# Hybrid encoder trunk on one core: attention weights of the third token group turned by VectorE's 32 by 32 block transposes and SBUF transfers instead of TensorE products

## The chip, the cores and the metric

The kernel runs on one core of a Trainium2 chip. The metric is the device time of one execution in microseconds (us). The engines are named as in the profile: PE is TensorE (PEld its weight loads), DVE is VectorE, ACT is ScalarE, POOL is GpSimd, SP is SyncE, which here only issues transfers; "SPq" is the issuing of one.

## What is computed

One layer of an encoder over 2048 prompt tokens and 8 x 16 sample tokens, width 1024, all in float32. One input projection feeds three branches (a short convolution, a gated linear recurrence, attention) and the merge gates; each branch is projected back, gated and added, and an output projection closes the layer. The part that the change touches is the attention of the prompt. It is "stick-breaking": no softmax, but for query q and key k (k before q) the weight is sigmoid(z) times the product of sigmoid(-z) over all keys between k and q.

```python
def sb_attend(q, k, v, q_pos, k_pos):
    z = jnp.einsum('bqhd,bkhd->bhqk', qf, kf) * (1.0 / math.sqrt(SB_DH))
    causal = (k_pos[None, :] < q_pos[:, None])[None, None]
    log_1mb = jnp.where(causal, jax.nn.log_sigmoid(-z), 0.0)
    rest = lax.cumsum(log_1mb, axis=3, reverse=True) - log_1mb
    A = jnp.where(causal, jnp.exp(jax.nn.log_sigmoid(z) + rest), 0.0)
    return jnp.einsum('bhqk,bkhd->bqhd', A, vf)
```

## The kernel before

Tokens come in 17 tiles of 128 (one of samples, 16 of the prompt), and the tiles in three groups (`GROUPS`, line 39). For each group, `run_jobs` (line 1319) goes through the columns of the input projection in jobs of 128 or 256 columns; each job is a chain of products into a PSUM buffer `acc` (lines 710 and 721), emptied by ScalarE or VectorE. After the third group comes the merge (`merge_jobs`, line 1398), whose products are at lines 1440 and 1471.

Other work is laid between these products by hand. Every generator that yields a cost is drained by a `Background` (line 58): after a few products of the main job the caller grants a budget, and the background runs until its yields have used it up. `hbg` runs the recurrence beside every group (`recurrence`, line 983): per pair of tiles and head seven levels, and in each VectorE makes two operands (`WR`, `WL`, lines 1028 and 1034) and updates `X` and `hgf` (1035, 1036), TensorE multiplies the operands into a PSUM buffer `z` (1039), and VectorE copies a masked part of that into the scores `sc` (1040). Before the first level VectorE multiplies `qk` (999), TensorE sums it into a `z`, and VectorE starts `sc` from it (1004). `bg` runs the attention of the prompt, beside the third group at rate 0.65 (0.3 of that in jobs of 256 columns) and beside the merge at rate 1.

The attention (`attn_pair`, line 297) takes 512 queries (four blocks of 128) and two heads at a time, from the latest keys back, in segments of up to 512 keys. For one segment and one head it makes a step, for each of the four query blocks a turn:

- TensorE: z = Q Kt in two products (lines 329, 330), into one of two `z` buffers, which the recurrence uses as well;
- ScalarE: sigmoid(-z) into one of three buffers `snb` (333), sigmoid(z) into one of four `sp` (335); on the diagonal GpSimd masks both (338);
- VectorE: the running product along the keys by a scan into one of two buffers `pr` (342), continued over segments through `carry` (346, GpSimd), then `sp` = `sp` x `pr` (347), the weights, with queries on partitions;
- three turns later (`queue`, `shorten`, `DEPTH`): TensorE turns the weights so that keys are on partitions, by one product with an identity per 128 x 128 block (line 310) into PSUM `tp`, and ScalarE copies them into `aT` (311).

When both heads of a segment are turned, `accumulate` (line 352) multiplies `aT` by the values `Vt` into the PSUM buffer `pv` (359). At the end of a pair of heads `store` (364) multiplies `pv` by a gate `ot` that was loaded from DRAM (320, 366), splits the result into two parts (`oth` and `ot`, in `store_parts`, line 178) and stores both to `OX` by SyncE.

All transfers but the indirect ones are issued from SyncE's queue. A tile framework places the waits and the order of each engine's instructions; eight semaphores, DMAHW0 to DMAHW7, are given to the transfers in turn.

Of the kernel before, what the change touches and what calls it, by code (L numbers as in the profile page):

```python
# [8 lines left out]
F32 = mybir.dt.float32  # L9
# [7 lines left out]
P = 128  # L17
# [81 lines left out]
def trunk(ctx: ExitStack, tc: tile.TileContext, x_prompt, x_sample, cache_conv, state_hgrn, cache_k, cache_v,  # L99
# [140 lines left out]
    at = None  # L240
    snb = []
    turn = [0]

    def open_attention():

        nonlocal at
        at = ctx.enter_context(tc.tile_pool(name="at", bufs=2, side="right"))

        for i in range(3):
            s = at.tile([P, 513], F32, name=f"snb{i}", bufs=1)  # L250
            nc.vector.memset(s[:, 512:513], 1.0)
            snb.append(s)


# [13 lines left out]
    def load_step(m):  # L268
# [20 lines left out]
        if e == 0:  # L289
            Vt = at.tile([P, 4, 2, 64], F32, tag="Vt", name="Vt")  # L290
            nc.sync.dma_start(Vt[:, :nb], VV[(1 + b0) * P:(1 + b1) * P, h:h + 2].rearrange(
                "(b p) e c -> p b e c", p=P))
        else:
            Vt = held[m - 1][3]
        held[m] = (Q1, Q2, Kt, Vt)

    def attn_pair(m0, m1):
# [8 lines left out]
        def transposed(i, e, w, sp, aT):  # L306
            nb = w // P
            tp = ps_tp()
            for j in range(nb):
                nc.tensor.transpose(tp[:, j * P:(j + 1) * P], sp[:, j * P:(j + 1) * P], idf)  # L310
            nc.scalar.copy(aT[:, e, 0:nb, i * P:(i + 1) * P], tp[:, :w].rearrange("p (b q) -> p b q", q=P))  # L311

        gate = []
        for m in range(m0, m1):
            _, _, si, last, b0, b1, e = steps[m]
            load_step(m)
            load_step(m + 1)
            if m == m1 - 1:
                gate.append(at.tile([P, 512], F32, tag="ot", name="ot", bufs=1))
                nc.sync.dma_start(gate[0][:, :n], SZ[pair][:, q0:q0 + n])  # L320
            Q1, Q2, Kt, Vt = held[m]
            nb = b1 - b0
            diag = si == 0
            if e == 0:
                aT = at.tile([P, 2, 4, 512], F32, tag="aT", name="aT", bufs=1)
            for i in range(nq):
# [25 lines left out]
            def accumulate(nb=nb, diag=diag, first=si == 0, last=last, Vt=Vt, aT=aT):  # L352
                if first:
                    box.append(ps_pv())
                pv = box[0]
                for j in range(nb):
                    c0 = j * P if diag else 0
                    for e in range(2):
                        nc.tensor.matmul(pv[64 * e:64 * e + 64, c0:n], Vt[:, j, e], aT[:, e, j, c0:n],  # L359
                                         start=first and j == 0, stop=last and j == nb - 1, skip_group_check=True)  # L360
# [1171 lines left out]
```

## Time and profile before

| what | us |
|---|---|
| time, median of 3 runs (2873.08 to 2874.37) | 2874.01 |
| the profiled execution: its own time | 2876.11 |
| its span, first to last instruction | 2873.2 |
| TensorE busy | 2853.0 |
| VectorE busy | 1546.5 |
| ScalarE busy | 1018.7 |
| GpSimd busy | 331.8 |

A row of a group reads: line, engine, operation, output <- input, shapes, count | busy us in all, mean ns of one | idle time of the engine just ahead of it, and what ended most of that. A matmul's busy time overlaps with its neighbours', so a group's busy time isn't what TensorE would save without it. A row by stretch gives its start and end, its length, each engine's busy us with the number of instructions, the clock granted to TensorE (1.00 is full), the mean busy share of the 16 DMA engines, and what they moved in GB/s. In the chain of waits a piece is work that the end of the run hung on. A row of transfers gives the issuing queue, the count, the size and the median time from issue to landing.

### The profile page before, as it was taken

Reading aid. Unit: us, or ns where it says so; the run is one execution under the profiler, and the core shown is the slowest. Engines: PE = TensorE matmul, PEld = TensorE weight load, DVE = VectorE, ACT = ScalarE, POOL = GpSimd, SP = SyncE. Lnnn points to the kernel's source line nnn. Section 1 sums busy time; section 2 is a strip of 40 time slices with the busy share of each in tenths; the row PEclk is TensorE's granted clock in tenths of the full one; section 3 lists DMA queues with packets and bytes.
Section 4 is the critical chain, followed back from the end, with each engine's and each line's share of the span. In section 5 each row is a group of like instructions: output and inputs, shape, how many; then the busy total and the mean of one; then the engine's idle time right before and its main releaser. Section 6 shows DMA issues by size and latency. Waiting matters only on the chain.

```text
span 2873.2 us, 51723 instructions
## 1 busy us (share of the span) xinstructions
PE 2853.0 (99%) x19479; PEld 2662.3 (93%) x19479; DVE 1546.5 (54%) x3304; ACT 1018.7 (35%) x2375; POOL 331.8 (12%) x802
## 2 busy tenths in 40 slices
PE   9999999999999999999999999999999999999999
PEld 9999999999999999999999999999998888787888
DVE  5454635641344442545434747557485876867743
ACT  4333222242233332213334444434444444544420
POOL 3110000111200000001323111111010011010100
PEclk9999999999999999999999999999999999999999
DMA  8887777777678887746766454544447877878876
GB/s 306 305 276 247 231 241 244 231 243 243 212 249 266 276 265 243 243 167 192 237 215 202 146 173 136 173 139 151 144 145 238 286 234 239 266 250 266 271 250 210
DMA packets 370475, 649.76 MB, mean 226 GB/s; under 512 B 33481, under 2 KB 246306, under 8 KB 339506
## 3 DMA queue, kind: packets, MB, share of 16 engines
q1 hardware_dynamic: 369458, 644.36, 68.2%
q8 instruction: 154, 2.52, 0.4%
q0 software_dynamic: 768, 2.10, 0.2%
q14 instruction: 95, 0.78, 0.1%
HBM read 447.06 MB, written 199.27 MB: 225 GB/s over the span
## 4 chain that ended last, share of the span: by engine, by line
PE 76%; DVE 2%; DMA 2%; issue 1%; ACT 0%; POOL 0%; SPq 0%; DVEq 0%; POOLq 0%; ACTq 0%
PE acc L710 33%; PE acc L721 10%; PE acc L1440 9%; PE acc L1471 6%; PE pv L359 4%; PE tp L310 4%; PE z L330 2%; PE z L329 2%; PE z L1039 1%; PE tp L458 1%; DMA gate<-GM 1%; PE pv L522 1%; PE z L476 0%; PE hg L1086 0%; PE hg L826 0%
## 5 line engine op out<-in xcount | busy, mean ns | idle before, releaser
L710 PE MATMUL acc<-hx,w 128*128 128x384 f32 (+1 forms) x6816 | 1251.8, 333 | 0.1
L710 PEld LDWEIGHTS acc<-hx,w 128*128 128x128 f32 x6816 | 1106.5, 188 | 21.9 <-issue 15.2
L721 PE MATMUL acc<-w,hx 128*128 128x256 f32 x2544 | 328.6, 284 | 1.8 <-DVE hx L176 0.9
L342 DVE TENSOR_TENSOR_SCAN pr<-snb,carry 128x513 f32<-128x513 f32 x192 | 246.5, 1284 | 153.3 <-ACT snb L333 151.7
L721 PEld LDWEIGHTS acc<-w,hx 128*128 128x128 f32 x2544 | 310.9, 188 | 5.0 <-DVE hx L176 1.7
L311 ACT COPY aT<-tp 128x512 f32<-128x512 f32 (+2 forms) x320 | 167.6, 524 | 375.2 <-PE tp L310 361.3
L710 PE MATMUL acc<-hx,wst 128*128 128x384 f32 x1248 | 247.2, 344 | 0.0
L1440 PE MATMUL acc<-o,w 128*128 128x512 f32 (+2 forms) x1080 | 234.7, 363 | 1.8 <-DMA o<-OX 1.8
L333 ACT ACTIVATE snb<-z 128x512 f32<-128x512 f32 (+2 forms) x320 | 172.4, 539 | 144.5 <-PE z L330 140.4
L710 PEld LDWEIGHTS acc<-hx,wst 128*128 128x128 f32 x1248 | 215.4, 188 | 6.4 <-issue 3.7
L1440 PEld LDWEIGHTS acc<-o,w 128*128 128x128 f32 x1080 | 185.1, 188 | 33.8 <-issue 5.3
L347 DVE TENSOR_TENSOR sp<-sp,pr 128x512 f32<-128x512 f32 (+2 forms) x320 | 195.3, 611 | 29.2 <-POOL sp L338 3.7
L342 DVE TENSOR_TENSOR_SCAN pr<-snb,one 128x129 f32<-128x129 f32 (+3 forms) x128 | 114.4, 894 | 123.9 <-POOL snb L338 123.6
L310 PE MATMUL tp<-idf,sp 128*128 128x128 f32 x1088 | 171.3, 273 | 2.5 <-ACT aT L311 1.5
L335 ACT ACTIVATE sp<-z 128x512 f32<-128x512 f32 (+2 forms) x320 | 171.5, 536 | 0.0
L1471 PE MATMUL acc<-w,mh 128*128 128x256 f32 x816 | 161.2, 285 | 1.0 <-DVE yt L1479 0.8
L1176 ACT ACTIVATE gm<-acc 128x384 f32<-128x384 f32 (+1 forms) x144 | 68.2, 474 | 230.4 <-PE acc L710 197.5
L310 PEld LDWEIGHTS tp<-idf,sp 128*128 128x128 f32 x1088 | 131.8, 141 | 19.3 <-issue 4.4
L176 DVE TENSOR_TENSOR w<-wst,w 128x1024 fp32r<-128x1024 f32 x72 | 88.1, 1223 | 110.7 <-ACT w L175 107.9
L1471 PEld LDWEIGHTS acc<-w,mh 128*128 128x128 f32 x816 | 131.0, 188 | 7.2 <-issue 4.2
L329 PE MATMUL z<-Kt,Q 128*128 128x512 f32 (+2 forms) x320 | 128.8, 403 | 0.3 <-ACT sp L335 0.2
L359 PE MATMUL pv<-aT,Vt 128*64 128x512 f32 (+3 forms) x640 | 128.1, 535 | 0.0
(299 smaller groups left out, 3570.1 us busy)
## 6 DMA issues: line engine op xcount, KB each, us to landing
w<-W SPq DMA_DIRECT2D x168, 1024.0 KB, 6.0
W<-w SPq DMA_DIRECT2D x72, 1024.0 KB, 5.0
wst<-W SPq DMA_DIRECT2D x112, 512.0 KB, 5.1
wst<-in_w_in_dram SPq DMA_DIRECT2D x72, 512.0 KB, 5.1
GM<-gm SPq DMA_DIRECT2D x120, 192.0 KB, 3.7
W<-mwp SPq DMA_DIRECT2D x40, 512.0 KB, 4.2
Kt<-KT SPq DMA_DIRECT2D x160, 128.0 KB, 3.1
o<-OX SPq DMA_DIRECT2D x72, 256.0 KB, 4.7
```

The costliest lines, as they stand in the source:

```text
L310: nc.tensor.transpose(tp[:, j * P:(j + 1) * P], sp[:, j * P:(j + 1) * P], idf)
L311: nc.scalar.copy(aT[:, e, 0:nb, i * P:(i + 1) * P], tp[:, :w].rearrange("p (b q) -> p b q", q=P))
L329: nc.tensor.matmul(z[:, :w], Q1[:, i * P:(i + 1) * P], Kt[:, :w], start=True, stop=False)
L333: nc.scalar.activation(sn[:, 512 - w:512], z[:, :w], AF.Sigmoid, scale=-0.125)
L335: nc.scalar.activation(sp[:, :w], z[:, :w], AF.Sigmoid, scale=0.125)
L342: nc.vector.tensor_tensor_scan(pr[:, 512 - w:513][:, ::-1], s_in, s_in, one if diag else carry[e][i], ALU.mult, ALU.bypass)
L347: nc.vector.tensor_tensor(sp[:, :w], sp[:, :w], pr[:, 513 - w:513], ALU.mult)
L359: nc.tensor.matmul(pv[64 * e:64 * e + 64, c0:n], Vt[:, j, e], aT[:, e, j, c0:n], start=first and j == 0, stop=last and j == nb - 1, skip_g ...
L710: nc.tensor.matmul(acc[:, :n], w[0][a][:, k], hT[b][:, k, :n], start=k == 0 and i == 0, stop=k == KB - 1 and i == 2)
L721: nc.tensor.matmul(acc[:, :256], hT[b][:, k, ti * P:(ti + 1) * P], w[k // 4][a][:, k % 4], start=k == 0 and i == 0, stop=k == KB - 1 and i ...
L1440: nc.tensor.matmul(acc[:, :n], w[0][a][:, k, dd * P:(dd + 1) * P], box[x][b][:, k, sl], start=k == 0 and i == 0, stop=k == 3 and i == 2)
L1471: nc.tensor.matmul(acc[:, :256], box["l" if b else "h"][:, k, ti * P:(ti + 1) * P], w[k // 4][a][:, k % 4], start=k == 0 and i == 0, stop= ...
```

## The change

In the third token group, not in the merge, the weights are turned in another way. VectorE transposes the 32 by 32 blocks of `sp` in place of TensorE, into a new buffer `T` (one, for the four turns of a step). That leaves each block turned, but not at the partitions where it belongs. So after the fourth turn 16 transfers, SBUF to SBUF, of 32 partitions each (64 KB) carry the blocks to their partitions in `aT`; eight are issued by ScalarE's queue, eight by SyncE's. `aT` has another layout for that, and in the merge ScalarE's copy writes this layout too.

Other things change with it. The accumulation of a segment waits in `pending` and joins the queue two turns into the next segment; the store as well; at the end of 512 queries a yield of 5.0 stands ahead of the rest. `Vt` has one buffer instead of two and is loaded in the third turn of the second head. The gate `ot` and the part `oth` no longer have buffers of their own but take those of `pr`, and the gate is loaded with the last accumulation. There are two buffers `snb` instead of three. Costs that the turns yield are the same as before.

```diff
-        for i in range(3):
+        for i in range(2):
             s = at.tile([P, 513], F32, name=f"snb{i}", bufs=1)
...
+        turned_.append(at.tile([P, 4, 4, 4, 32], F32, name="T", bufs=1))
+        nc.gpsimd.memset(turned_[0], 0.0)
...
-            nc.scalar.copy(aT[:, e, 0:nb, i * P:(i + 1) * P], tp[:, :w].rearrange("p (b q) -> p b q", q=P))
+            nc.scalar.copy(aT[:, e, i, :, 0:nb], tp[:, :w].rearrange("p (b a q) -> p a b q", a=4, q=32))
+
+        def turned_blocks(i, e, w, sp, aT):
+
+            T = turned_[0]
+            nc.vector.transpose(T[:, i, :, 0:w // P].rearrange("p c b q -> p b c q"),
+                                sp[:, :w].rearrange("p (b c q) -> p b c q", c=4, q=32))
+            if i == nq - 1:
+                for a in range(4):
+                    for c in range(4):
+                        queue_ = nc.scalar if (a + c) % 2 else nc.sync
+                        queue_.dma_start(aT[32 * c:32 * c + 32, e, :, a], T[32 * a:32 * a + 32, :, c])
...
-            if m == m1 - 1:
-                gate.append(at.tile([P, 512], F32, tag="ot", name="ot", bufs=1))
-                nc.sync.dma_start(gate[0][:, :n], SZ[pair][:, q0:q0 + n])
...
             if e == 0:
-                aT = at.tile([P, 2, 4, 512], F32, tag="aT", name="aT", bufs=1)
+                aT = at.tile([P, 2, 4, 4, 4, 32], F32, tag="aT", name="aT", bufs=1)
+                turn_ = turned_blocks if by_blocks[0] else transposed
+                if not by_blocks[0]:
+                    queue.extend(pending)
+                    pending.clear()
...
-                queue.append((True, lambda i=i, e=e, w=w, sp=sp, aT=aT: transposed(i, e, w, sp, aT)))
+                queue.append((True, lambda i=i, e=e, w=w, sp=sp, aT=aT, f=turn_: f(i, e, w, sp, aT)))
+                if e == 0 and i == 1:
+
+                    queue.extend(pending)
+                    pending.clear()
+                if e == 1 and i == 2:
+                    Vt = at.tile([P, 4, 2, 64], F32, tag="Vt", name="Vt", bufs=1)
...
+                if last:
+                    gate.append(at.tile([P, 513], F32, tag="pr", name="ot", bufs=2))
+                    nc.sync.dma_start(gate[0][:, :n], SZ[pair][:, q0:q0 + n])
...
-                        nc.tensor.matmul(pv[64 * e:64 * e + 64, c0:n], Vt[:, j, e], aT[:, e, j, c0:n],
+                        nc.tensor.matmul(pv[64 * e:64 * e + 64, c0:n], Vt[:, j, e],
+                                         aT[:, e, c0 // P:nq, :, j].rearrange("p i a q -> p (i a) q"),
                                          start=first and j == 0, stop=last and j == nb - 1, skip_group_check=True)
             if e:
-                queue.append((False, accumulate))
+                (pending if turn_ is turned_blocks else queue).append((False, accumulate))
...
-            th = at.tile([P, 512], F32, tag="oth", name="oth", bufs=1)
+            th = at.tile([P, 513], F32, tag="pr", name="oth", bufs=2)
             store_parts(OX[2, pair], slice(q0, q0 + n), t[:, :n], th[:, :n])
-        queue.append((False, store))
+        (pending if turn_ is turned_blocks else queue).append((False, store))
...
         yield from shorten(0)
+        if pending:
+            yield 5.0
+            queue.extend(pending)
+            pending.clear()
+            yield from shorten(0)
...
     tpools.close()
+    by_blocks[0] = False
```

In the changed kernel the lines above are numbered anew: 999, 1004, 1028, 1034, 1035, 1036, 1039 and 1040 of the recurrence become 1028, 1033, 1057, 1063, 1064, 1065, 1068 and 1069, the scan 354, the multiply 359, the block transpose 316, the transfers 322.

More of the change, by code (lines that the diff above doesn't have):

```diff
@@ L241, in trunk @@
     snb = []
+    turned_ = []
+    by_blocks = [True]
+    pending = []
     turn = [0]
@@ L288, in load_step @@
                               KT[pair, v, 64 * e:64 * e + 64, (1 + b0) * P:(1 + b1) * P].bitcast(F32))
[L289 to L295, printed above, removed]
+        held[m] = (Q1, Q2, Kt)
     def attn_pair(m0, m1):
@@ L317, in attn_pair @@
             load_step(m + 1)
-            if m == m1 - 1:
-                gate.append(at.tile([P, 512], F32, tag="ot", name="ot", bufs=1))
-                nc.sync.dma_start(gate[0][:, :n], SZ[pair][:, q0:q0 + n])
-            Q1, Q2, Kt, Vt = held[m]
+            Q1, Q2, Kt = held[m]
             nb = b1 - b0
@@ L348, in attn_pair, with accumulate @@
                 yield 1.7 * w / 512
-                queue.append((True, lambda i=i, e=e, w=w, sp=sp, aT=aT: transposed(i, e, w, sp, aT)))
+                queue.append((True, lambda i=i, e=e, w=w, sp=sp, aT=aT, f=turn_: f(i, e, w, sp, aT)))
[4 more added lines that the diff above has]
+                    Vt = at.tile([P, 4, 2, 64], F32, tag="Vt", name="Vt", bufs=1)
+                    nc.sync.dma_start(Vt[:, :nb], VV[(1 + b0) * P:(1 + b1) * P, 2 * pair:2 * pair + 2].rearrange(
+                        "(b p) e c -> p b e c", p=P))
                 yield from shorten(DEPTH)
-            def accumulate(nb=nb, diag=diag, first=si == 0, last=last, Vt=Vt, aT=aT):
+            def accumulate(nb=nb, diag=diag, first=si == 0, last=last, Vt=Vt if e else None, aT=aT):
                 if first:
                     box.append(ps_pv())
+                if last:
+                    gate.append(at.tile([P, 513], F32, tag="pr", name="ot", bufs=2))
+                    nc.sync.dma_start(gate[0][:, :n], SZ[pair][:, q0:q0 + n])
                 pv = box[0]
```

## The prediction

> **What bounds the kernel now.** I read the page first, for the span and the engines' busy time, then the busy time by stretch, then the groups and the chain of the third token group alone, and last VectorE's order of time in one of its dense places. The page:
>
> ```profile
> span 2873.2 us, 51723 instructions
> PE 2853.0 (99%) x19479; PEld 2662.3 (93%) x19479; DVE 1546.5 (54%) x3304; ACT 1018.7 (35%) x2375; POOL 331.8 (12%) x802
> ```
>
> TensorE never rests, so a product that goes shortens the run, as long as nothing else makes TensorE wait. The change works where the third token group's projections and the attention run side by side, from about 1340 to 2180 us. Busy time in that stretch, then in the four stretches of it in which the recurrence runs as well (columns: PE, PEld, DVE, ACT, POOL, clock, DMA share, GB/s):
>
> ```profile
> 1340.00:2180.00 840.00, 836.45 (x5422) 782.00 (x5420) 487.22 (x1049) 340.98 (x851) 149.28 (x348) 1.00 0.53 171
> sum 320.00, PE 318.66 PEld 297.38 DVE 254.06 ACT 130.70 POOL 43.31; mean PE 79.66 PEld 74.34 DVE 63.52 ACT 32.68 POOL 10.83
> ```
>
> TensorE is idle for 3.5 of 840 us, at full clock; VectorE is busy 58% over all (487 of 840), but 79% (254 of 320) beside the recurrence. The groups of instructions in 1340 to 2180, largest shapes apart where it matters:
>
> ```profile
> L310 PE MATMUL tp<-idf,sp 128*128 128x128 f32 x508 | 81.6, 273 | 0.6 <-DVE sp L347 0.6
> L311 ACT COPY aT<-tp 128x512 f32<-128x512 f32 (+3 forms) x159 | 79.5, 500 | 165.1 <-PE tp L310 163.8 <-PE z L329 1.0
> L347 DVE TENSOR_TENSOR sp<-sp,pr 128x512 f32<-128x512 f32 (+3 forms) x161 | 93.6, 582 | 15.1 <-POOL sp L338 3.7
> L347 DVE TENSOR_TENSOR sp<-sp,pr 128x512 f32<-128x512 f32 x95 | 65.7, 692 | 9.2 <-POOL sp L338 2.6
> L342 DVE TENSOR_TENSOR_SCAN pr<-snb,carry 128x513 f32<-128x513 f32 x73 | 93.8, 1285 | 79.6 <-ACT snb L333 78.6
> ```
>
> 508 transposing products stand in the stretch, in 160 turns (one turn: one block of 128 queries of one head against up to 512 keys). The chain of waits from 1340 to 2185, by line, and one piece of it:
>
> ```profile
> by line: PE acc L710 53.2%; PE acc L721 16.3%; PE pv L359 6.5%; PE tp L310 6.1%; PE z L330 3.4%; PE z L329 3.3%; PE z L1039 2.0%; DVE pr L342 0.8%; PE hg L1086 0.7%; PE hg L826 0.6%; DMA xt<-in_x_prompt_dram 0.6%; DMA o<-OX 0.6%; PE tp L108
> 1667.27 0.44 PE tp L310 x4
> ```
>
> The chain is TensorE almost alone, and the products to be removed hold 6.1% of 845 us in it.
>
> **What goes.** 0.061 x 845 = 51.5 us, or 0.101 us for each of 508; the piece says 0.11. The 81.6 us of the group count the overlap of pipelined products with their neighbours, so I take 51.5, with 56 (508 x 0.11) as the other end. ScalarE's 160 copies go too (79.5 us), off the path: ScalarE is busy 341 of 840 us.
>
> **What comes to VectorE.** 160 block transposes, one a turn. No such instruction is in the trace. Nearest rows: the multiply of the same width, 0.692 us, and the scan, 1.285. I take the multiply, since a transpose too reads and writes each element once: 160 x 0.582 = 93 us, which makes VectorE 580 of 840. Away from the recurrence that is hidden in its idle time. Beside the recurrence it isn't all hidden. VectorE in time there:
>
> ```profile
> 1648.41 1.29 DVE L342 TENSOR_TENSOR_SCAN pr<-snb,one 128x513 f32<-128x513 f32 x1 [1.39 <-POOL snb L338]
> ...
> 1658.44 1.28 DVE L342 TENSOR_TENSOR_SCAN pr<-snb,carry 128x513 f32<-128x513 f32 x1
> ...
> 1660.43 0.29 DVE L1040 COPY_PREDICATED sc<-lmask,z 128x128 f32<-128x128 int32 x1
> ```
>
> From 1648.4 to 1660.7 no instruction of it has an idle time before it. Every level of the recurrence goes VectorE, TensorE (line 1039), VectorE, and TensorE takes its instructions in order. How the transposes stand among them, on VectorE where the recurrence of head 0's first pair of tiles begins (WR, WL, X and hgf are its operands, pr the scan, sp the weights, sc the scores). Before:
>
> ```order
> L999 TENSOR_TENSOR qk<-hgq,hgk 128x256
> L1028 TENSOR_TENSOR WR<-hgq,hgf 128x2x64
> L1036 TENSOR_TENSOR hgf<-hgf 128x2x64
> L1028 TENSOR_TENSOR WR<-hgq,hgf 128x2x32x2
> L1035 TENSOR_TENSOR X<-X,hgf 128x2x32x2
> L1036 TENSOR_TENSOR hgf<-hgf 128x2x32x2
> L342 SCALAR_TENSOR_TENSOR pr<-snb_15445,carry 128x513
> L347 TENSOR_TENSOR sp<-sp,pr 128x512
> L1004 TENSOR_TENSOR sc<-idf,z 128x256
> ```
>
> The same place now, from the first transpose to sc:
>
> ```order
> L1057 TENSOR_TENSOR WR<-hgq,hgf 128x2x64
> L316 STREAM_TRANSPOSE T<-sp 128x2x4x32
> L1065 TENSOR_TENSOR hgf<-hgf 128x2x64
> L1063 TENSOR_TENSOR WL<-hgk,X 128x2x32x2
> L1057 TENSOR_TENSOR WR<-hgq,hgf 128x2x32x2
> L1064 TENSOR_TENSOR X<-X,hgf 128x2x32x2
> L316 STREAM_TRANSPOSE T<-sp 128x3x4x32
> L354 SCALAR_TENSOR_TENSOR pr<-snb_15445,carry 128x513
> L1065 TENSOR_TENSOR hgf<-hgf 128x2x32x2
> L359 TENSOR_TENSOR sp<-sp,pr 128x512
> L316 STREAM_TRANSPOSE T<-sp 128x4x4x32
> L1033 TENSOR_TENSOR sc<-idf,z 128x256
> ```
>
> A whole step's transposes (the first, of one block, stands just ahead of these rows) come together in front of sc, which frees the buffer z for TensorE's next product. The order has 55 of the 160 inside the 12 runs of levels. In the four stretches VectorE then works 254 + 55 x 0.692 = 292 of what would be 320 - 55 x 4 x 0.101 = 298 us: 98%, with in-order partners. I followed these rows by hand: TensorE waits 1.3 to 1.5 us at sc, and little further on. 12 x 1.5 = 18 us. Ends: 0 if the spare is used fully; with the scan's price 254 + 55 x 1.285 = 325, that is 27 us more than TensorE has, and 18 on top: 45.
>
> [...]
>
> **What comes to the queues.** Each step (four turns) sends its turned megabyte by 16 transfers of 32 partitions, eight on ScalarE's queue, eight on SyncE's: 640 in 40 steps. ScalarE's order, at the start of the same head's recurrence, names the semaphores waited for. Before:
>
> ```order
> L311 COPY aT<-tp 128x4x128 [waits PE_49]
> L1224 ACTIVATE hgf<-acc 128x2x128 [waits PE_49]
> L1224 ACTIVATE hgf<-acc 128x128
> L1226 ACTIVATE hgk<-acc 128x2x128
> L333 ACTIVATE snb_15445<-z 128x512 [waits DVE_49,PE_49]
> ```
>
> Now:
>
> ```order
> L1255 ACTIVATE hgk<-acc 128x128
> L322 DMA aT<-T 32x4x128 [waits DMAHW5_49,DMAHW6_49,DMAHW4_49,DVE_49]
> L345 ACTIVATE snb_15445<-z 128x128 [waits PE_49,Pool_49]
> L347 ACTIVATE sp<-z 128x128
> L322 DMA aT<-T 32x4x128 [waits DMAHW5_49]
> L322 DMA aT<-T 32x4x128 [waits DMAHW6_49]
> L322 DMA aT<-T 32x4x128 [waits DMAHW0_49]
> L345 ACTIVATE snb_15447<-z 128x256 [waits PE_49,Pool_49]
> ```
>
> The copies' place is taken by transfers that wait for earlier transfers: eight semaphores, DMAHW0 to 7, serve both queues in turn, so a transfer starts when the one eight before it has landed. Queued behind such a wait on ScalarE are the sigmoids of z and the emptying of acc, which TensorE waits for; on SyncE the loads of w, Kt and Q; on VectorE the next step's first transpose, since T is one buffer. Nearest rows, in us from issue to landing and for issuing alone:
>
> ```profile
> KT<-kt SPq DMA_DIRECT2D x68, 128.0 KB, 4.2
> OX<-oth SPq DMA_DIRECT2D x16, 256.0 KB, 2.4
> 1609.67 0.32 SPq L208 DMA_DIRECT2D w<-W  x1
> 1612.54 0.59 SPq L281 DMA_DIRECT2D Q<-QT  x1
> ```
>
> Two rounds of eight take 2 x 2.4 to 2 x 4.2, plus the issue of eight at 0.32 to 0.59: 7 to 13 us. A turn is 840 / 160 = 5.25 us on average, and the order leaves two to three turns from a step's last transpose to the next step's first, 10.5 to 16. So mostly hidden; ScalarE gains 8 x 0.45 = 3.6 us of issuing a step where four copies took 2. I charge 0.25 us a step, 10 us; ends 0 and 2 us a step (80).
>
> **Small edits.** ot and oth now sit in the scan's two pr buffers and the gate is loaded with the last accumulation, so a pair's next scan waits for OX stores: 2.4 us after the cast in the row above. The sigmoid buffers are two, not three; Vt is one. TensorE has 24 and more products queued at a pair's end. 16 pairs x 0.4 = 6 us; ends 0 and 16 x 2.4 = 38. The order keeps 508 blocks in the third group, so the merge that follows has as many transposing products as before; only aT's layout differs there. The later due time of accumulations moves work, and costs nothing.
>
> **The sum.** -51.5 + 18 + 10 + 6 = -17.5 us. The profiled execution took 2876.1 us for its span of 2873.2, 2.1 above the median 2874.0 of the runs; taken from the median: 2856.5 us.
>
> **The rivals.**
> 1. All of it is hidden: TensorE waits nowhere more than now. For it: TensorE's slack at most places, VectorE 58% busy. Against: 98% beside the recurrence. 2874.0 - 51.5 = 2822.5.
> 2. VectorE becomes the bound, because the transpose costs what the scan costs. Then 45 in place of 18: -51.5 + 45 + 10 + 6 = +9.5, 2883.5. It decides from a stall of 35 us, about 1.0 us a transpose. Against it: nothing in the transpose depends on the element before it.
> 3. The transfers become the bound (slower): the chain of 16 through eight semaphores, among loads of w, outlasts the two turns, and VectorE stands at the first transpose with the scan and the recurrence behind it, or ScalarE with the sigmoids. It decides from (51.5 - 18 - 6) / 40 = 0.7 us a step; at 1.3 us, 52 in place of 10: +24.5, 2898.5. For it: in 1340 to 2180 the transfers are already 53% busy, and 13 us against 10.5 is within my bounds. [...]
> 4. It does not do what it says: the time freed on TensorE reappears as its waits elsewhere, term for term. 2874.
>
> **How the numbers follow.** The forecast 0.34, rival 1 0.20, rival 2 0.12, rival 3 0.22, rival 4 0.12. A difference of 0.2% (5.7 us) is about what can be told from none. Faster by more: forecast and rival 1, 0.54; within: rival 4 and nothing else, 0.12; slower: rivals 2 and 3, 0.34. The range reaches from rival 1 (2822) to a little past rival 3 (2902): 8 in 10, since the transfers' upper end lies beyond. For a faster outcome alone it would be 2822 to 2868.
>
> **What would show it.** L310's counterpart with 580 products, all after the third group; transposes near 0.69 us; TensorE's idle time in the third group growing from 3.5 us to about 30, behind sc and VectorE in the recurrence. Wrong if the waits of ScalarE or VectorE for DMA carry more than 30 us of TensorE's idle time, if transposes take 1 us, or if the merge's part changes by more than 10 us.

## The result, and the profile after

The changed kernel takes 2915.65 us (median of 4 runs, 2911.14 to 2917.59) against 2874.19 of the kernel before: ratio 1.0142, 95% interval 1.0124 to 1.0159. It is slower by 41.5 us; the forecast was 2856.5 and the range ended at 2902. The page of the profiled execution (2914.1 us):

```profile
span 2912.4 us, 51541 instructions
PE 2841.4 (98%) x18971; PEld 2626.5 (90%) x18971; DVE 1608.7 (55%) x3463; ACT 942.6 (32%) x2215; POOL 333.5 (11%) x803
PE 60%; DMA 7%; DVE 6%; issue 3%; SPq 2%; ACT 1%; POOL 1%; ACTq 1%; DVEq 0%; POOLq 0%
```

The 508 products are gone (19479 to 18971), and TensorE's busy time fell by only 11.6 us. In the chain of the whole span (third row) TensorE now holds 60%, where it held 76%, and transfers and queues 7 + 2 + 1%. Where the time went shows by stage. Third group with attention, then merge, cut at the merge's first product (columns as in the prediction: length, PE, PEld, DVE, ACT, POOL, clock, DMA share, GB/s). Before:

```profile
1340.00:2182.90 842.90, 837.15 (x5427) 782.47 (x5425) 489.99 (x1052) 343.19 (x854) 149.28 (x348) 1.00 0.53 171
2182.90:2873.20 690.30, 684.18 (x4294) 578.60 (x4294) 448.37 (x636) 258.76 (x518) 56.91 (x192) 1.00 0.77 254
```

After:

```profile
1340.00:2201.80 861.80, 811.58 (x4886) 738.44 (x4885) 537.72 (x1190) 260.39 (x679) 142.09 (x343) 0.98 0.71 210
2201.80:2912.40 710.60, 698.76 (x4328) 587.68 (x4328) 462.88 (x658) 265.83 (x533) 64.46 (x197) 0.99 0.78 254
```

The third group lost 18.9 us, the merge 20.3. In the third group TensorE is busy 25.6 us less, but idle 50.2 us (861.80 less 811.58) where it was 5.8; the clock granted to it fell to 0.98. The chain of waits of this stretch, which the prediction found to be TensorE almost alone:

```profile
by line: PE acc L739 27.8%; DMA aT<-T 8.8%; PE acc L750 8.3%; issue 5.3%; PE pv L382 5.0%; DVE pr L354 4.0%; DVE T L316 3.1%; DMA wst<-W 2.9%; SPq L322 2.9%; ACTq L322 2.1%; DVE sp L359 2.0%; DMA Q<-QT 1.7%; PE z L341 1.7%; PE z L342 1.6%; 
```

The transfers' landing holds 8.8% of it, their issuing by SyncE and ScalarE 2.9 and 2.1%: some 119 of 861.8 us. The groups that answer to the prediction's, of the same stretch of the changed kernel (first row: VectorE's transposes of full width; second: the sigmoids on ScalarE, behind the bar their idle time before and what ended it), then ScalarE's and SyncE's transfers over the whole span:

```profile
L316 DVE STREAM_TRANSPOSE T<-sp 128x512 f32<-128x512 f32 x86 | 58.5, 694 | 3.8 <-DMA aT<-T 2.2 <-DMA w<-W 1.2 <-issue 0.3
L345 ACT ACTIVATE snb<-z 128x512 f32<-128x512 f32 (+3 forms) x157 | 80.3, 511 | 214.2 <-PE z L342 109.8 <-DMA aT<-T 61.5 <-DVE T L316 9.3
```

```profile
L322 ACTq DMA_DIRECT2D aT<-T x320: 592/612/1749, 1355.6 to 2249.2; - x160
L322 SPq DMA_DIRECT2D aT<-T x320: 585/604/2190, 1357.2 to 2249.5; - x160
DMA to landing us min/median/max: 2.0/2.3/7.6
```

The transpose costs what the prediction took, 0.694 us. New is what stands before the sigmoids: 61.5 us that end with the landing of a transfer. (This is ScalarE's idle time; what of it TensorE waited for, these rows don't tell.) The same group before had next to nothing but z to wait for:

```profile
L333 ACT ACTIVATE snb<-z 128x512 f32<-128x512 f32 (+3 forms) x164 | 85.1, 519 | 78.6 <-PE z L330 76.3 <-DVE sc L1040 1.4
```

And issuing one transfer takes its queue 0.61 us, by the rows of the transfers. In order of time, a bad place of the changed kernel:

```profile
1453.38 5.64 SPq L322 DMA_DIRECT2D aT<-T  x8
1460.73 1.10 DVE L316 STREAM_TRANSPOSE T<-sp 128x128 f32<-128x128 f32 x3 [11.06 <-DMA aT<-T]
1460.76 3.89 PE L382 MATMUL pv<-aT,Vt 128*64 128x512 f32 x14 [2.39 <-DMA aT<-T]
...
1466.08 8.70 ACTq L322 DMA_DIRECT2D aT<-T  x6
...
1474.82 0.37 ACT L864 COPY vf<-acc 128x256 f32<-128x256 f32 x1 [8.55 <-DMA Q<-QT]
...
1475.24 1.69 PE L750 MATMUL acc<-wst,hx 128*128 128x256 f32 x12 [0.69 <-ACT vf L864]
```

SyncE issues eight transfers in 5.6 us, VectorE has stood 11.1 us for T, TensorE waits for the landing, and then ScalarE is held 8.7 us by six transfers; vf, which empties an accumulator, comes after that, and TensorE waits for it. What let ScalarE go on was the landing of Q, a load of SyncE's: the eight semaphores ("lanes" from here on) tie the two queues together.

ScalarE also stands for a buffer. `aT` has one, so the transfers of a new segment must wait until the values' products of the segment before, which are now due later, have read it:

```profile
2133.48 3.97 PE L382 MATMUL pv<-aT,Vt 128*64 128x512 f32 x16
2137.48 2.68 ACTq L322 DMA_DIRECT2D aT<-T  x4
2140.54 0.60 ACT L345 ACTIVATE snb<-z 128x512 f32<-128x512 f32 x1 [9.82 <-PE z L342]
```

The first transfer goes out when the sixteen products end, 6.8 us after ScalarE's last work. (TensorE has no idle time beside this one; it has other work.) By the semaphores that came last in the trace, ScalarE's issues waited 37 us in 12 stands for these products, 22 us in 25 for an earlier transfer to land, and 13 us in 6 for VectorE's transposes.

### The profile page after: what moved, and what is told of

Its sections match the earlier page's. It is cut to its first block, busy times and chain, and to the rows that moved or that the text cites. A ratio compares the mean times of both kernels' runs of the same rounds, so it can differ in the third digit from the quotient of the medians.

```text
span 2912.4 us, 51541 instructions
## 1 busy us (share of the span) xinstructions
PE 2841.4 (98%) x18971; PEld 2626.5 (90%) x18971; DVE 1608.7 (55%) x3463; ACT 942.6 (32%) x2215; POOL 333.5 (11%) x803
## 4 chain that ended last, share of the span: by engine, by line
PE 60%; DMA 7%; DVE 6%; issue 3%; SPq 2%; ACT 1%; POOL 1%; ACTq 1%; DVEq 0%; POOLq 0%
PE acc L739 24%; PE acc L1470 8%; PE acc L750 7%; PE acc L1501 7%; PE pv L382 4%; DMA aT<-T 3%; PE tp L310 2%; PE z L342 1%; PE z L341 1%; DVE pr L354 1%; PE tp L487 1%; PE z L1068 1%; DVE T L316 1%; DMA wst<-W 1%; SPq L322 1%
## 5 line engine op out<-in xcount | busy, mean ns | idle before, releaser
L311 ACT COPY aT<-tp 128x512 f32<-128x512 f32 (+3 forms) x160 | 87.6, 550 | 182.6 <-PE tp L310 163.7
L382 PE MATMUL pv<-aT,Vt 128*64 128x512 f32 (+3 forms) x640 | 141.4, 542 | 2.4 <-DMA aT<-T 2.4
L341 PE MATMUL z<-Kt,Q 128*128 128x512 f32 (+2 forms) x320 | 127.3, 399 | 9.6 <-ACT sp L347 4.8
L342 PE MATMUL z<-Kt,Q 128*128 128x512 f32 (+2 forms) x320 | 117.1, 366 | 0.0
L1501 PE MATMUL acc<-w,ml 128*128 128x256 f32 x408 | 115.0, 282 | 0.0
```

Source lines behind the costliest of these rows:

```text
L341: nc.tensor.matmul(z[:, :w], Q1[:, i * P:(i + 1) * P], Kt[:, :w], start=True, stop=False)
L342: nc.tensor.matmul(z[:, :w], Q2[:, i * P:(i + 1) * P], Kt[:, :w], start=False, stop=True)
L1501: nc.tensor.matmul(acc[:, :256], box["l" if b else "h"][:, k, ti * P:(ti + 1) * P], w[k // 4][a][:, k % 4], start=k == 0 and i == 0, stop= ...
```

## The experiments

Theory A: the transfers cost (rival 3). B: VectorE's load beside the recurrence costs. C: the small edits cost. All kernels start from the changed one. Lengths by stage are cut as above.

**1. What remains without block turns.**

```diff
-    by_blocks = [True]
+    by_blocks = [False]
```

> The third group's weights go through TensorE's products again, as in the kernel before; everything else of the change stays: the new layout of the turned weights, two buffers of the sigmoids in place of three, one buffer of the values, the gate and the output's parts in the buffers of the products' scan, the later loads of the values. Theory A (the sixteen transfers a step are what costs): these small edits cost about what the prediction put on them, so 2874 to 2890 us. Theory B (VectorE's added transposes beside the recurrence cost): the same, 2874 to 2890 us, since no transpose is left on VectorE. Theory C (the small edits cost, above all the third buffer that is gone): 2900 us or more, and with it most of the 20 us that the merge lost.

2877.38 us, ratio to the kernel before 1.0011 (1.0001 to 1.0020): the small edits cost 3.5 us. C falls.

**2. Block turns without transfers.**

```diff
-            nc.vector.transpose(T[:, i, :, 0:w // P].rearrange("p c b q -> p b c q"),
+            nc.vector.transpose(aT[:, e, i, :, 0:w // P].rearrange("p c b q -> p b c q"),
...
-            if i == nq - 1:
-                for a in range(4):
...
-                (pending if turn_ is turned_blocks else queue).append((False, accumulate))
+                queue.append((False, accumulate))
```

> VectorE's transposes write straight into the tile that the values' products read, and the sixteen transfers are left out: each 32 by 32 block is turned but stays in its own 32 partitions, so the attention's output of the third group is not the reference's. The values' products follow at once, as in the kernel before. Theory A (transfers cost): the gain comes out that the prediction had without its 10 us for transfers, about 2847 us, anywhere from 2825 to 2860. Theory B (VectorE's load costs): 2880 us or more. Theory C (small edits cost): 2900 us or more.

2837.42 us, 0.9876 (0.9859 to 0.9892). A holds and B falls. The stage rows of the third group, with products kept, and then with block turns without transfers:

```profile
1340.00:2184.50 844.50, 837.34 (x5425) 782.19 (x5423) 489.00 (x1052) 343.10 (x854) 149.52 (x348) 1.00 0.53 170
```

```profile
1340.00:2142.90 802.90, 790.51 (x4923) 732.55 (x4922) 562.27 (x1212) 269.55 (x694) 150.62 (x348) 1.00 0.56 180
```

TensorE's busy time falls by 46.8 us and its idle time rises from 7.2 to 12.4: that is all that 73 us more work on VectorE costs. So the transfers, with the deferral that they need, cost 2915.65 - 2837.42 = 78.2 us, 1.96 a step.

**3. One, four, sixteen.** The same megabyte a step in one transfer, in four by two queues, in four by SyncE:

```diff
+                nc.sync.dma_start(aT[:, e], T)
```

```diff
+                for j in range(4):
+                    queue_ = nc.scalar if j % 2 else nc.sync
+                    queue_.dma_start(aT[:, e, j], T[:, j])
```

```diff
+                for j in range(4):
+                    nc.sync.dma_start(aT[:, e, j], T[:, j])
```

> The sixteen transfers of 64 KB by two queues become one transfer of 1 MB by SyncE, all 128 partitions straight across: the same bytes in the same place of the order, the same waits of the transposes and of the values' products, but one issue and one semaphore lane a step. The blocks stay in their own partitions, so the attention's output of the third group is not the reference's. Theory A in the form that issuing and the eight lanes cost (ScalarE and SyncE held up): within 15 us of the kernel without transfers, 2840 to 2865 us. Theory A in the form that moving the bytes or the time to landing costs (T's one buffer and the turned tile's wait): 2885 us or more. Theory B: as without transfers, 2880 us or more.

> Four transfers of 256 KB a step, straight across all 128 partitions, two by each queue, where the changed kernel has sixteen and the kernel of one transfer one. The blocks stay in their own partitions, so the attention's output of the third group is not the reference's. If each transfer costs alike (issue), the time lies on the line from 2845 us at one to 2916 us at sixteen, 4.7 us for each transfer more: 2859 us. If the round over eight lanes is what costs (a ninth transfer waits for the first to land), four stay under it: 2852 us or less. If ScalarE's part alone counts, two of eight issues: 2863 us.

> Four straight transfers of 256 KB a step, all by SyncE, none by ScalarE; the blocks stay in their own partitions, so the attention's output of the third group is not the reference's. Theory D in ScalarE's form (the 19 us over one transfer are ScalarE standing still until VectorE's transpose is done): 2852 us or less. Theory I (each issue costs, by whichever queue): 2864 us or more.

One: 2845.09 us, 0.9900 (0.9883 to 0.9916). Four by SyncE: 2851.39, 0.9921 (0.9905 to 0.9938). Four by two queues: 2864.47, 0.9964 (0.9950 to 0.9978). The bytes, T's single buffer and the deferral together cost 7.7 us over no transfer, nearly all of it in the merge (690.7 to 698.9). Three more issues on SyncE cost 6.3. Two of four moved to ScalarE cost 13.1. The four by SyncE lie where they were expected if ScalarE's part counts (2852 or less), not where each issue costs alike (2864 or more); the four by two queues are nearest to ScalarE's part too (2863), but 2859 for each issue alike is only 5 us off. ScalarE stands at a transfer until VectorE has turned the block, and until the values' products have read `aT`: in the trace of the four by two queues 43 us in 24 stands and 50 us in 16. Waits of the kernel with four by two queues, then with four by SyncE (total, times, longest):

```profile
DVE T L316 <- DMA aT<-T: 48.7, 25, 6.7
ACT snb L344 <- DVE T L316: 9.0, 3, 3.6
ACT hgq L1261 <- DVE T L316: 6.1, 2, 4.8
ACT gm L1204 <- DVE T L316: 4.3, 1, 4.3
```

```profile
DVE T L316 <- DMA aT<-T: 20.1, 13, 8.4
ACT sp L345 <- DVE T L316: 4.0, 4, 1.7
```

**4. All sixteen by one queue.**

```diff
-                        queue_ = nc.scalar if (a + c) % 2 else nc.sync
+                        queue_ = nc.sync
```

and so with nc.scalar and nc.gpsimd.

> All sixteen transfers a step are issued by SyncE, none by ScalarE; nothing is left out. If ScalarE's time is what costs (eight issues of 0.61 us a step and the lane waits in front of the sigmoids), the time falls by 15 us or more, to 2900 us or less. If the loads that SyncE issues late are what costs (the weights of the branches, keys and queries behind sixteen issues and their lane waits), it rises by 5 us or more, to 2920 to 2960 us. Theory B and C: within 5 us of the changed kernel.

> All sixteen transfers a step are issued by ScalarE, none by SyncE; nothing is left out. If late loads of SyncE are what costs the changed kernel its time: 2900 us or less. If ScalarE's standing still costs (16 issues of 0.61 us and the lane waits ahead of the next sigmoids, 10 to 16 us a step): 2950 us or more. With both alike, about 2916 us. SyncE alone gave 3024 us.

> All sixteen transfers a step are issued by GpSimd, which is busy 11% of the span; nothing is left out. Theory A1 (what costs is that ScalarE and SyncE, which issue the transfers, stand still: sigmoids, evictions and loads come late): the time falls to 2850 to 2880 us, below the kernel before at the lower end. Theory A2 (what costs is the transfers themselves: sixteen of 128 pieces of 512 bytes each, and the time until the last has landed, whoever issues them): 2900 us or more. A third way: GpSimd's issue takes longer than the 0.6 us of the other two, and the masks of the diagonal jobs and the carries, GpSimd's own, come late in the recurrence: more than 2916 us.

SyncE: 3023.79 us, 1.0520 (1.0498 to 1.0542). ScalarE: 3110.39, 1.0819 (1.0797 to 1.0841). GpSimd: 2996.19, 1.0433 (1.0415 to 1.0451). Each queue alone is far worse than two. SyncE alone was expected at 2960 us at most and missed that by 64; the ranges met by the other two had no upper end. With sixteen on ScalarE the sigmoids wait 222 us for transfers; with sixteen on GpSimd, whose issue takes 0.55 us, the landing lengthens (median 4.9 us, 2.3 in the changed kernel) and VectorE waits 75.2 us for T. From the tables on the transfers, ScalarE's kernel and GpSimd's:

```profile
  ACT snb L345: 222.0, 22
```

```profile
L322 POOL DMA_DIRECT2D aT<-T x640: 551/551/688, 1353.8 to 2331.5; - x160
  DVE T L316: 75.2, 18
DMA to landing us min/median/max: 1.9/4.9/9.4
```

SyncE has spare time to lose, and it shows in what SyncE itself waits for. With one transfer, in 1340 to 2200, its loads of w waited 84.9 us for their buffer to come free; in the changed kernel 38.9:

```profile
SPq L208 <- PE acc L736: 84.9, 18, 11.6
```

```profile
SPq L208 <- PE acc L739: 38.9, 9, 14.1
```

With all sixteen by SyncE no such wait is left among its twelve largest, and VectorE waits 81.7 us for T and TensorE for w (14.9 and 13.4): SyncE's own stream had become the late one.

**5. Transfers beside the products.** The products turn the weights, and idle transfers go beside them, from a constant into a tile that nobody reads:

```diff
-    by_blocks = [True]
+    by_blocks = [False]
...
+                G = g_bc.rearrange("p (i f) -> p i f", i=4)
+                for a in range(4):
+                    for c in range(4):
+                        queue_ = nc.scalar if (a + c) % 2 else nc.sync
+                        queue_.dma_start(turned_[0][32 * c:32 * c + 32, :, a].rearrange("p i b q -> p i (b q)"),
+                                         G[32 * a:32 * a + 32, :, 0:128])
```

then with `0:1` for both `:` over i (a quarter of the bytes), and with only the odd or only the even a + c.

> TensorE's products turn the weights as in the kernel with the products kept (2877 us), and beside them the sixteen transfers a step are issued, by both queues in turn and at the same place, but from a constant into a tile that nobody reads: the same pieces and bytes, and nothing that they wait for or that waits for them but the lanes. Nothing of the computation is left out. Theory I (the issue and the eight lanes cost, whatever is moved): they cost here what they cost the changed kernel over the one without transfers, 78 us: 2940 to 2960 us. Theory D (the dependency costs: ScalarE and SyncE stand at a transfer until VectorE's transpose is done, VectorE stands until the transfers have read T, the products until they have landed): 2880 to 2900 us.

> As the sixteen idle transfers a step beside the products (2933 us, 56 over the kernel with the products kept), but each of 16 KB in 32 pieces of 512 bytes instead of 64 KB in 128: the same sixteen issues and lanes, a quarter of the pieces and bytes. Nothing of the computation is left out. If the issue's 0.6 us on its queue is what costs: 2925 to 2940 us. If it is the pieces, and with them how long a lane stays taken: 2905 us or less.

> Of the sixteen idle transfers a step beside the products only ScalarE's eight, SyncE's eight are not issued. Nothing of the computation is left out. If ScalarE's standing still costs: 2915 us or more, most of the 56 us. If both queues alike: 2900 to 2910 us. If what costs is the ninth to sixteenth on the eight lanes, wherever they are: 2890 us or less, and the same for SyncE's eight.

> Of the sixteen idle transfers a step beside the products only SyncE's eight. Nothing of the computation is left out. If ScalarE's standing still was what cost: 2880 to 2890 us here. If SyncE's stream (loads of the branches' weights, keys and queries that come late) costs: 2905 us or more. If only more than eight a step cost: 2890 us or less, as with ScalarE's eight.

The idle transfers go beside 38 steps. All sixteen: 2933.01 us, 1.0193 (1.0173 to 1.0214), 55.6 over the products kept and between the two expectations. A quarter of the bytes: 2939.05, 1.0222 (1.0205 to 1.0240), no less: bytes and pieces aren't what idle transfers cost. ScalarE's eight alone: 2916.05, 1.0143 (1.0126 to 1.0160), 38.7 over. SyncE's eight alone: 2882.26, 1.0027 (1.0015 to 1.0040), 4.9 over. The third group with all sixteen, with ScalarE's eight, and with SyncE's:

```profile
1340.00:2241.80 901.80, 858.82 (x5426) 795.40 (x5424) 489.50 (x1052) 340.67 (x854) 148.03 (x348) 0.98 0.70 204
```

```profile
1340.00:2222.70 882.70, 847.57 (x5423) 786.68 (x5421) 489.37 (x1051) 340.65 (x854) 146.83 (x348) 0.99 0.61 185
```

```profile
1340.00:2191.50 851.50, 839.94 (x5423) 783.77 (x5421) 489.46 (x1051) 341.91 (x854) 147.73 (x348) 1.00 0.63 192
```

These transfers wait for nothing but the lanes, and nothing waits for them; yet they cost 56 us, 39 of it with ScalarE's eight alone. ScalarE has 0.6 us for each issue, and a lane wait where the eighth transfer before has not landed: with its eight alone, idle time of 21.3 us ahead of kt and of 20.0 ahead of aT ended with the landing of an idle transfer. But the idle transfers don't stand where the changed kernel's stand. With no data to wait for they come earlier, ScalarE's above all (ScalarE's eight alone, then SyncE's):

```profile
L320 ACTq DMA_DIRECT2D T<-g_bc x304: 592/593/1670, 1334.5 to 1736.4; - x152
L320 SPq DMA_DIRECT2D T<-g_bc x304: 585/600/2325, 1355.7 to 2013.9; - x152
```

ScalarE issues its 304 within 402 us, where its 320 of the changed kernel take 894 us (1355.6 to 2249.2), and SyncE its 304 within 658. They are scattered, too: 199 of the 216 groups in which ScalarE's stand among its other instructions are of one or two. So the 56 us are no part that can be taken out of the 78, the two queues are compared at unequal rates, and the loss needs no burst of eight. It depends on the place: of the 35.1 us that TensorE is idle beside ScalarE's eight, 30.9 lie before 1640 us, though transfers go on until 1736. TensorE's longest waits are for kt (11.1 us), kn (7.9) and vf (5.3), short jobs of that stage that go through ScalarE.

How issue and lane wait share ScalarE's 39 us was not told apart, since the smaller transfers took nearly as long to land (median 2.5 us against 2.9).

**6. One job later.**

```diff
+                if i == nq - 1 and turn_ is turned_blocks:
+                    queue.append((False, lambda e=e, aT=aT: placed(e, aT)))
```

with the two loops over a and c in `placed`.

> The sixteen transfers of a step are issued one place later in the attention's queue, behind the next job, when VectorE's transposes have long been done; nothing is left out. Theory D (standing still for VectorE's transposes costs): 2860 to 2895 us. Theory I (issue and lanes): 2905 to 2925 us, as the changed kernel.

2906.56 us, 1.0113 (1.0096 to 1.0130): 9 us less, between the two expectations and nearer to issue and lanes. ScalarE's sigmoids still wait 37.0 us for transfers (61.5 in the changed kernel). The added place in the queue also slows the attention: 36 of the 40 steps are turned by blocks in this kernel (144 transposes), the other four move into the merge, so its stages don't compare, and its total only roughly.

**7. Through DRAM.** Five transfers a step, one out and four back; then the reads and products two jobs later; then the values' load behind those reads.

```diff
+                nc.sync.dma_start(TD[e], T)
+        def placed(e, aT):
+            for c in range(4):
+                nc.sync.dma_start(aT[32 * c:32 * c + 32, e],
+                                  TD[e].rearrange("(a x) i c b q -> c x i a (b q)", a=4)[c])
```

```diff
+                if i == 1:
+                    queue.extend(reads_)
+                    reads_.clear()
...
-                if e == 0 and i == 1:
+                if e == 0 and i == nq - 1:
```

```diff
+                if e == 1 and i == nq - 1 and turn_ is turned_blocks:
+                    reads_.append((False, lambda vt=vt, b0=b0, b1=b1, nb=nb: load_values(vt, b0, b1, nb)))
```

> The blocks are put in place through DRAM: one straight transfer of 1 MB out, and, one place later in the attention's queue, four of 256 KB back, each into 32 partitions, all issued by SyncE; five transfers a step instead of sixteen, and nothing is left out. If the number of transfers is what costs: 2845 us plus 4 x 4.7 = 2864 us, below the kernel before. If SyncE stands still until the part written has landed (two to four us in each of 40 steps, with the loads of the branches behind it): 2890 us or more. Theory A2 (bytes and time to land): 2916 us or more, since twice the bytes move.

> As the way through DRAM, but the four transfers back are issued two jobs later (behind the second job of the next head), the values' products two jobs later too, and the values are loaded one job later. Nothing is left out. SyncE's 83 us of standing still for the part written should go. If those waits were what cost: 2850 to 2870 us, below the kernel before. If twice the bytes in pieces of 512 bytes, or five issues a step in SyncE's stream, cost: 2940 us or more.

> As the way through DRAM with the later reads (2995 us), but the load of the values, for which SyncE stood 99 us until the products of the step before were done, is issued behind the next step's reads, when its buffer has long been free. Nothing is left out. If that wait in SyncE's stream was the loss: 2900 us or less, at the best 2860 us, below the kernel before. If the bytes are (2 MB more a step beside the loads, landing of 5 to 7 us where one inside SBUF takes 2.3): within 30 us of 2995 us.

2988.41 us, 1.0396 (1.0379 to 1.0413); 2995.14, 1.0418 (1.0400 to 1.0435); 2975.44, 1.0361 (1.0343 to 1.0379). The expectation of about 2860 us failed three times. (As in 6, only 36 of the 40 steps are turned by blocks in these three, 144 transposes.) The waits for the written part fell from 83.4 us to 26.5 without a gain, and the values' load, moved, gave 20 us. The count of transfers isn't all, then: five a step through DRAM cost more here than sixteen inside SBUF. The loads of w land later beside it. Transfers in the third group of the last of the three, and of the changed kernel (KB each, median us to landing):

```profile
w<-W SPq DMA_DIRECT2D x52, 1024.0 KB, 8.1
TD<-T SPq DMA_DIRECT2D x33, 1024.0 KB, 8.1
aT<-TD SPq DMA_DIRECT2D x132, 256.0 KB, 5.4
```

```profile
w<-W SPq DMA_DIRECT2D x54, 1024.0 KB, 6.0
aT<-T ACTq DMA_DIRECT2D x304, 64.0 KB, 2.5
```

That the bytes are the cause there is only argued; which of the late loads holds the 100 us stays open.

**8. ScalarE relieved.** The odd eight by GpSimd in place of ScalarE, at once and one job later (the edits of 4 and 6 together).

> The changed kernel with ScalarE's eight transfers a step issued by GpSimd; SyncE keeps its eight; nothing is left out. If ScalarE's standing still is what costs the changed kernel most (39 us of idle issues and some of the 13 us of waiting for VectorE's transposes), and GpSimd's half costs little: 2855 to 2872 us, below the kernel before. If GpSimd's standing still holds up the masks and carries of the recurrence as with all sixteen on it (2996 us), half of that: 2890 to 2920 us.

> The same, with the transfers one place later in the attention's queue, so that neither SyncE nor GpSimd stands until VectorE's transposes are done; nothing is left out. If that wait matters for GpSimd, 5 to 15 us below the run with the transfers at the first place; if only the issues count, within 5 us of it.

2897.65 us, 1.0080 (1.0063 to 1.0097), and 2897.17, 1.0078 (1.0062 to 1.0095). Taking ScalarE's eight away gains 18.0 us on the changed kernel, less than the 39 of the idle ones. The sigmoids' waits for transfers are gone, but GpSimd's eight cost too. The second of the two turns only 36 steps by blocks, so the equal times don't show what the wait for VectorE costs. Waits in the third group with SyncE and GpSimd at the first place:

```profile
ACT snb L345 <- PE z L342: 165.4, 87, 10.7
POOL aT L322 <- PE pv L382: 58.7, 8, 17.8
POOL aT L322 <- DVE T L316: 30.5, 7, 9.8
PE z L341 <- DVE sc L1069: 8.9, 7, 6.9
```

GpSimd stands at its transfers, until the products have read aT and until VectorE has turned the block, and TensorE waits 8.9 us for the recurrence's sc where it waited 3.6 in the changed kernel. How GpSimd's share of the loss splits was not tried. At the first place the third group is back at 844.3 us, but the merge is still at 713.3. No version that leaves nothing out beat the kernel before.

## Why the prediction was wrong

The sum by its own terms, with what each measured:

| term | predicted us | measured us | from |
|---|---|---|---|
| products gone, with VectorE's stalls | -51.5 + 18 = -33.5 | -40.0 | no transfers less products kept |
| transfers | +10 (0 to 80) | +78.2 | changed kernel less no transfers |
| small edits | +6 (0 to 38) | +3.5 | products kept less before |
| sum | -17.5 | +41.7 (41.5 measured) | |

**The step that failed** is the transfers' price: "Two rounds of eight take 2 x 2.4 to 2 x 4.2 ... So mostly hidden; ScalarE gains 8 x 0.45 = 3.6 us of issuing a step where four copies took 2. I charge 0.25 us a step." It compared the landing with the average turn, as if only VectorE's wait for T mattered. Shown in its place: the transfers cost 78.2 us, 1.96 a step. The landing hides well when one transfer of the same bytes does it (7.7 us in all). Eight issues a step on ScalarE cost 39 us though they carry nothing, eight on SyncE 5, each at the places that they took, and ScalarE's eight given to GpSimd gained 18. That ScalarE was busy only 341 of 840 us hid the point: part of its spare time lies between short jobs that TensorE waits for, and standing 8.7 us at six transfers doesn't fit there. The prediction weighed ScalarE's issuing (3.6 us a step against 2) and charged 0.25 us a step for everything else, with it ScalarE's stands ahead of an issue: for a lane, for VectorE's transposes, for `aT`. How the 78.2 us split between issuing and these waits stays open. 13.1 us for two of four transfers moved to ScalarE and the 22.6 us above the idle transfers (7.7 of it the deferral) come from kernels that differ in more than that, and no run gave `aT` or `T` a second buffer.

**The prices.** The issue was 0.61 us, not 0.45; both rows used were of transfers over more partitions. The transpose was right at 0.692 (0.694), and rival 2 with it wrong. The row of its narrowest form:

```profile
L316 DVE STREAM_TRANSPOSE T<-sp 128x128 f32<-128x128 f32 x22 | 6.6, 300 | 16.4 <-DMA aT<-T 14.4 <-DMA Kt<-KT 1.9
```

From 128 columns (0.300 us) to 512 (0.694) a column costs 1.03 ns, and some 0.17 us are fixed: an estimate from these two rows. 256 and 384 columns took 0.406 and 0.550 us in the same trace. The stall beside the recurrence was put at 18 us and came to 5.2 of idle time without transfers, so the fear of VectorE at 98% was too large. The products gave 46.8 us of busy time against 51.5.

**The rivals.** Rival 3 had the right mechanism and named ScalarE with its sigmoids as one of the two places, but it was priced at 1.3 us a step; it was 1.96. The text's own bound, 2 us a step, would have given 2874.0 - 51.5 + 18 + 80 + 6 = 2926.5; the range stopped at 2902, a little past rival 3's 2898.5, and said that this upper end lies beyond it, at 8 in 10. Rival 2's turning point is 1.1 us a transpose by the sum's own terms (254 + 55 x 1.11 = 315, 17 us over 298), not 1.0; that changes nothing here.

**The second queue.** Issuing a transfer took 0.61 us against 2.3 to landing, and yet the second queue was worth 108 us and more: 2916 us by two queues, 3024 and 3110 by one. The sum has no term for it.

**The merge.** "The later due time of accumulations moves work, and costs nothing" failed too, and with it the test of 10 us: the merge lost 20.3. With one transfer it already loses 8.2 against none (698.9, 690.7), and it has 34 more products than before (4328, 4294), 16 of them by the values and 14 for z: products of the attention's last steps now stand in the merge. Of the 20.3 us, 14.6 are TensorE's busy time and 5.7 its idle time; what else makes them wasn't told apart. Its first 50 us of the changed kernel, and the rest:

```profile
2201.80:2251.80 50.00, 44.59 (x247) 39.94 (x248) 29.63 (x45) 10.43 (x19) 0.92 (x5) 0.90 0.81 252
2251.80:2912.40 660.60, 654.17 (x4083) 547.74 (x4081) 433.25 (x614) 255.40 (x514) 63.54 (x192) 1.00 0.78 254
```

5.4 us of idle time and a clock of 0.90 stand at its start (before: no idle time in its first 50 us, at full clock), where the last transfers (until 2249.5) still run.

Right were: 580 products left, all after the third group; the transpose's price; the small edits; and the place that the test "wrong if the waits of ScalarE or VectorE for DMA carry more than 30 us" named, though how much of TensorE's idle time these waits carry isn't shown.

## What to carry to other kernels

Price a DMA by what it takes from the engine that issues it, in the order in which that engine works: number of issues times the issue's own row, plus its wait for the data, for the lane and for the buffer that it writes; ScalarE, busy 341 of 840 us in the kernel before, had no room for that here, where TensorE waited for its short jobs. Before products are exchanged for data movement, try the movement with nothing to move: eight idle transfers a step on the queue in question cost 39 us here. But look in the trace where they stand, since ScalarE's idle ones, which wait for no data, were all issued by 1736 us here, the changed kernel's by 2249. A range that ends short of a bound of its own sum leaves out a case that the sum has priced.

## What the hardware showed that was not expected

**With idle time on TensorE came a lower clock.** With the same products (5425 and 5426), sixteen idle transfers raised TensorE's idle time in the third group from 7.2 to 43.0 us and its busy time from 837.3 to 858.8, 21.5 of the 57.3 us. The mean granted clock of the profiled execution is 0.999 with the products alone and 0.994 beside these transfers; over 2934 us the difference is some 15 of the 21.5, an estimate, and what makes the rest isn't shown. At the place shown above, TensorE stood 2.4 us until 1460.76; the granted clock of the changed kernel then, in steps of 2 us:

```profile
1458.00:1460.00 2.00, 0.36 (x3) 0.04 (x1) 0.00 (x0) 0.49 (x1) 0.00 (x0) 1.00 0.45 104
1460.00:1462.00 2.00, 1.25 (x4) 0.73 (x6) 1.27 (x5) 0.66 (x2) 0.44 (x2) 0.62 0.79 257
1462.00:1464.00 2.00, 2.00 (x9) 1.10 (x6) 0.96 (x3) 0.00 (x0) 0.19 (x1) 0.53 0.78 144
1464.00:1466.00 2.00, 1.42 (x7) 0.74 (x5) 0.00 (x0) 0.61 (x2) 0.05 (x1) 1.00 0.92 342
```

Inside the two rows below full clock it is half:

```profile
1460.60:1463.70 3.10, 2.94 (x10) 1.63 (x11) 2.23 (x6) 0.66 (x2) 0.63 (x2) 0.50 0.85 207
```

At 0.50 the rows of 0.62 and 0.53 are 1.5 + 1.9 = 3.4 us of half clock. The 2.39 us that TensorE stood there are its longest idle time in the 10 us ahead of the fall.

**Inside SBUF the issue took 0.47 to 0.61 us at every size tried.** On ScalarE 0.61 us for 64 KB over 32 partitions, 0.55 for 16 KB, 0.47 for 256 KB over 128 partitions; 0.60, 0.59 and 0.51 on SyncE, and 0.50 there for 1 MB in one transfer (medians).
